# The first load of a log-sum-exp kernel in packets of 4 KB

## The chip, the cores and the metric

The kernel runs on one core of one Trainium2 chip; the other cores are idle. The metric is the device time of one execution in microseconds (us). All views of the profile come from one profiled execution of the kernel.

## What is computed

```python
"x": np.random.randn(32, 512, 1024).astype(np.float32)

def reference(x):
    max_x = np.max(x, axis=-1, keepdims=True)
    return (max_x.squeeze(-1) + np.log(np.sum(np.exp(x - max_x), axis=-1))).astype(np.float32)
```

For each of 16,384 rows of 1024 floats this is the logarithm of the sum of the exponentials. The input is 64 MiB, the output 64 KiB.

## The kernel before

Each of the 128 partitions holds 128 rows. The first 112 rows of a partition are contiguous in HBM (`x_rows`), the last 16 as well (`x_rest`). A ring in SBUF has room for 48 rows for each partition (`RING`), 192 KB.

The list `LOADS` sets the work: 18 loads of 16, 16, 16, 16, 13.5, 12.5, 9 and so on down to 0.46875 rows for each partition, and for each load how its rows are summed. One load is one DMA over all 128 partitions, issued on the queue of SP (SyncE) in `load` (line 139 of the profile). Both sides of it are contiguous within a partition: the first load moves 16 rows, 65,536 bytes, into each partition, and is carried out in one packet for each partition, 128 packets, eight for each of the core's 16 DMA engines. Each DMA engine adds one packet of 4 bytes that counts up the load's semaphore `landed[i]`; 16 such counts make the load landed.

On a landed load ScalarE (ACT) takes the exponential in place (line 228). The maximum isn't subtracted beforehand: the kernel computes the plain sum, checks that every sum and the last row's inputs are in a safe range, and has a slow path for inputs that aren't, which this input doesn't take. The sums go three ways: VectorE (DVE) adds whole rows (`R`, line 239); GpSimd (POOL) first adds the halves of a row (`F`, line 233) and VectorE sums what is left (line 171); or VectorE adds halves and sums in one instruction a row (`T`, line 249). The very last row comes in two pieces (`Y`, `Z`) that ScalarE sums itself (line 202). Logarithms (lines 268, 279, 281), the checks on VectorE and TensorE, and two stores (lines 276, 285) end the kernel.

The order around the change is written out by hand. SP issues the loads in the order of the list, and before an issue `sp.wait` waits for whichever engine last used that part of the ring. Loads 1 to 3 fill the 48 rows and wait for nothing. Load 4 waits until VectorE has summed the first 16 rows. The first load is moved to the front of the program by `start_early`: it stands in SP's first block, ahead of the Drain and the start barrier of the engines, and is the first instruction of the span; loads 2 and 3 are issued behind that barrier.

Of the kernel before, what the change touches and what calls it, by code (L numbers as in the profile page):

```python
# [15 lines left out]
RING = 48  # L16
B = 16
LATE = 119

# [31 lines left out]
def kernel(  # L53
# [30 lines left out]
    def source(e0, size):  # L84
        assert e0 >= W * d or e0 + size <= W * d
        return x_rest[:, e0 - W * d : e0 - W * d + size] if e0 >= W * d else x_rows[:, e0 : e0 + size]
# [8 lines left out]
    def sbuf(name, cols, dtype=fp32, rows=P):  # L95
        return nc.alloc_sbuf_tensor(name, [rows, cols], dtype).ap()

    ring = sbuf("ring", RING * d)
# [35 lines left out]
    def load(i, here, done_before, size):  # L134
        for a, b, who, at in users:
            if a < here + size and b > here:
                sp.wait(who, at)
        users[:] = [u for u in users if not (u[0] < here + size and u[1] > here)]
        return nc.sync.dma_start(
            out=ring[:, here : here + size], in_=source(done_before, size)  # L140
        ).then_inc(landed[i], 16)

    def check_early():
        dve.wait(act, summed_by_act)
        dve.wait(dve, dve.n)
        dve.did(nc.vector.tensor_scalar(  # L146
            out=clamped[:, 0:LATE], in0=sumexp[:, 0:LATE],
            scalar1=LOW, scalar2=HIGH, op0=ALU.max, op1=ALU.min,
        ))
        dve.wait(dve, dve.n)  # L150
        dve.did(nc.vector.scalar_tensor_tensor(  # L151
            out=clamped[:, 0:LATE], in0=clamped[:, 0:LATE], scalar=0.0, in1=sumexp[:, 0:LATE],
            op0=ALU.bypass, op1=ALU.not_equal, accum_out=bad[:, 0:1],
# [4 lines left out]
    def add_up(c, who, **kw):  # L158
        pe.wait(*who)
        return pe.did(nc.tensor.matmul(count, lhsT=ones, rhs=sumexp[:, c : c + 1], **kw))  # L160
# [19 lines left out]
    here = 0  # L180
    early_sum = 0
    done_before = 0
# [3 lines left out]
    for i, (size, ops) in enumerate(loads):  # L186
# [3 lines left out]
        if any(q < here + size and q + t * d > here for _, t, q, _ in folded):  # L190
            reduce_folded()
        dma = load(i, here, done_before, size)
        first_load = first_load or dma.ins
        end = here + size
        done_before += size
        act.wait(landed[i], 16)
        for k, (how, s) in enumerate(ops):
            rows = ring[:, p : p + s * d].rearrange("p (c d) -> p c d", d=d)
            if how in "YZ":
# [3 lines left out]
                    out=last_exp[:, here - p : end - p], in_=ring[:, here:end], func=AF.Exp,  # L203
# [4 lines left out]
                here = end  # L208
# [5 lines left out]
            elif how == "A":  # L214
# [3 lines left out]
                    out=v, in_=v, func=AF.Exp, accum_out=sumexp[:, c : c + 1]  # L218
# [5 lines left out]
            else:  # L224
# [4 lines left out]
                here = upto  # L229
            if how == "F":  # L230
# [3 lines left out]
                    out=rows[:, :, 0:H], in0=rows[:, :, 0:H], in1=rows[:, :, H:d], op=ALU.add  # L234
                ))
                folded.append((c, s, p, at))
            elif how == "R":
                dve.wait(act, at)
                who = (dve, dve.did(nc.vector.reduce_sum(  # L239
                    out=sumexp[:, c : c + s], in_=rows, axis=AX.X  # L240
                )))
                users.append((p, p + s * d, *who))
            elif how == "T":
# [3 lines left out]
                for r in range(s):  # L247
                    lo = rows[:, r, 0:H]
                    who = (dve, dve.did(nc.vector.scalar_tensor_tensor(  # L249
                        out=lo, in0=lo, scalar=1.0, in1=rows[:, r, H:d],  # L250
                        op0=ALU.mult, op1=ALU.add, accum_out=sumexp[:, c + r : c + r + 1],
                    )))
                    users.append((p + r * d, p + (r + 1) * d, *who))
                    if c + r >= LATE:
                        add_up(c + r, who, start=False, stop=False)
            if how == "A" and c >= LATE:
                add_up(c, who, start=False, stop=False)
# [5 lines left out]
            p += s * d  # L263
            if c == LATE:

# [3 lines left out]
                    out=res[:, 0:W], in_=sumexp[:, 0:W], func=AF.Ln  # L269
# [12 lines left out]
        out=res[:, LAST:NC], in_=last_sum, func=AF.Ln, bias=sumexp[:, LAST:NC]  # L282
# [7 lines left out]
    dve.did(nc.vector.scalar_tensor_tensor(  # L290
        out=clamped[:, LATE:NC], in0=sumexp[:, LATE:NC], scalar=LOW,
        in1=sumexp[:, LATE:NC], op0=ALU.max, op1=ALU.not_equal, accum_out=bad[:, 1:2],
# [9 lines left out]
        out=over[:, 0:half], in0=last_piece[:, 0:half], scalar=CEILING,  # L302
# [16 lines left out]
    with nc.If(all_fine < 1):  # L319
# [5 lines left out]
        for c0 in range(0, NC, RING):  # L325
# [6 lines left out]
            for c1, c2 in ((c0, edge), (edge, c0 + s)):  # L332
                if c1 == c2:
                    continue
                nc.scalar.dma_start(
                    out=ring[:, (c1 - c0) * d : (c2 - c0) * d],
                    in_=source(c1 * d, (c2 - c1) * d),
# [4 lines left out]
                out=neg, in_=v, op=ALU.max, axis=AX.X, negate=True  # L342
# [3 lines left out]
                out=v, in0=v, in1=neg[:, :, None].to_broadcast([P, s, d])  # L346
# [5 lines left out]
                out=sumexp[:, c0 : c0 + s], in_=v, axis=AX.X  # L352
# [70 lines left out]
```

## Time and profile before

| | |
|---|---|
| time, median of two runs | 161.68 us (161.67 and 161.69) |
| span of the profiled execution, first to last instruction | 160.39 us |
| its own time | not listed apart from the two runs; median less span 1.29 us |
| busy ACT, DVE, POOL, PE | 114.5, 114.3, 37.3, 2.2 us |
| read from HBM | 67.11 MB, 419 GB/s over the span |
| ScalarE's wait for loads | 43.0 us in 8 waits, the longest 19.3 us |

The span is counted from SP's first instruction, the issue of the first load. Busy time of an engine doesn't count the issuing of DMAs. In a view by stretches the DMA share is the engine time of the packets that start in the stretch, divided by 16 engines times its length; a packet of 64 KB takes longer than a short stretch, so the share can be over 1 there. GB/s is counted in the same way. An entry of the DMA list gives the size of the load and the time from its issue to its landing.

### The profile page before, as it was taken

Reading aid. Unit: us, or ns where it says so; the run is one execution under the profiler, and the core shown is the slowest. Engines: PE = TensorE matmul, PEld = TensorE weight load, DVE = VectorE, ACT = ScalarE, POOL = GpSimd, SP = SyncE. Lnnn points to the kernel's source line nnn. Section 1 sums busy time; section 2 is a strip of 40 time slices with the busy share of each in tenths; the row PEclk is TensorE's granted clock in tenths of the full one; section 3 lists DMA queues with packets and bytes.
Section 4 is the critical chain, followed back from the end, with each engine's and each line's share of the span. In section 5 each row is a group of like instructions: output and inputs, shape, how many; then the busy total and the mean of one; then the engine's idle time right before and its main releaser. Section 6 shows DMA issues by size and latency. Waiting matters only on the chain.

```text
span 160.4 us, 219 instructions
## 1 busy us (share of the span) xinstructions
PE 2.2 (1%) x26; PEld 1.1 (1%) x26; DVE 114.3 (71%) x59; ACT 114.5 (71%) x31; POOL 37.3 (23%) x11
## 2 busy tenths in 40 slices
PE   0000000000000000000000000000000000000022
PEld 0000000000000000000000000000000000000011
DVE  0000000009999499994999859959999999999996
ACT  3000059990699708995099949991999989799996
POOL 0000000000000000000000994690004969891000
DMA  7996996996996996996999999999999999999992
GB/s 262 523 523 262 523 523 262 523 507 278 523 490 294 523 490 294 523 490 294 482 441 441 441 425 409 409 409 480 432 395 417 450 416 398 448 411 424 412 413 95
DMA packets 2881, 67.18 MB, mean 419 GB/s; under 512 B 576, under 2 KB 704, under 8 KB 1344
## 3 DMA queue, kind: packets, MB, share of 16 engines
q1 hardware_dynamic: 2880, 67.18, 97.7%
q14 instruction: 1, 0.01, 0.0%
HBM read 67.11 MB, written 0.07 MB: 419 GB/s over the span
## 4 chain that ended last, share of the span: by engine, by line
DMA 52%; ACT 28%; DVE 19%; issue 1%; PE 0%
DMA ring<-in_x_dram 52%; ACT ring L228 27%; DVE sumexp L239 15%; DVE sumexp L171 2%; DVE ring L249 1%; DVE over L301 0%; PE count L306 0%; ACT res L268 0%; DVE clamped L290 0%; DVE fine L308 0%; DVE sumexp L212 0%
## 5 line engine op out<-in xcount | busy, mean ns | idle before, releaser
L228 ACT ACTIVATE ring<-ring 128x16384 f32<-128x16384 f32 (+16 forms) x23 | 111.7, 4908 | 43.0 <-DMA ring<-in_x_dram 43.0
L239 DVE TENSOR_REDUCE sumexp<-ring 128x16 f32<-128x16384 f32 (+4 forms) x9 | 85.6, 9513 | 42.7 <-ACT ring L228 42.7
L233 POOL TENSOR_TENSOR ring<-ring 128x3072 f32<-128x3072 f32 (+3 forms) x7 | 37.1, 5313 | 107.3 <-ACT ring L228 107.3
L171 DVE TENSOR_REDUCE sumexp<-ring 128x6 f32<-128x3072 f32 (+3 forms) x7 | 18.4, 2656 | 0.0
L249 DVE SCALAR_TENSOR_TENSOR ring<-ring 128x512 f32<-128x512 f32 x15 | 9.6, 687 | 0.4 <-ACT ring L228 0.4
L125 ACT ACT_TABLE_LOAD x1 | 1.3, 1283 | 1.4 <-PEq L62 1.4
L156 PE MATMUL count<-far,bad 128*1 128x1 f32 x2 | 0.2, 164 | 153.2 <-DVE clamped L151 153.2
L160 PE MATMUL count<-sumexp,ones 128*1 128x1 f32 x18 | 1.6, 164 | 3.6 <-DVE ring L249 3.6
L249 DVE DVE_READ_ACCUMULATOR ring<-ring 128x1 f32 x15 | 1.2, 82 | 0.0
L202 ACT ACTIVATE last_exp<-ring 128x544 f32<-128x544 f32 (+1 forms) x2 | 1.2, 584 | 0.0
L126 DVE MEMSET ones<- 128x1 f32 x1 | 0.1, 59 | 1.5 <-PEq L62 1.5
L156 PEld LDWEIGHTS count<-far,bad 128*1 128x1 f32 x2 | 0.1, 80 | 153.2 <-DVE clamped L151 153.2
L160 PEld LDWEIGHTS count<-sumexp,ones 128*1 128x1 f32 x18 | 0.8, 80 | 4.5 <-DVE ring L249 4.5
L301 DVE SCALAR_TENSOR_TENSOR over<-ring 128x240 f32<-128x240 f32 x1 | 0.4, 404 | 0.0
L308 DVE TENSOR_SCALAR fine<-count 1x1 int32<-1x1 f32 x1 | 0.1, 147 | 0.3 <-PE count L306 0.3
L151 DVE SCALAR_TENSOR_TENSOR clamped<-clamped,sumexp 128x119 f32<-128x119 f32 x1 | 0.3, 283 | 0.0
L268 ACT ACTIVATE res<-sumexp 128x112 f32<-128x112 f32 x1 | 0.3, 279 | 0.0
L281 ACT ACTIVATE res<-last_sum,sumexp 128x1 f32<-128x1 f32 x1 | 0.3, 261 | 0.0
L202 ACT ACTIVATION_READ_ACCUMULATOR last_exp<-ring 128x1 f32 x2 | 0.3, 126 | 0.0
L146 DVE TENSOR_SCALAR clamped<-sumexp 128x119 f32<-128x119 f32 x1 | 0.2, 221 | 0.0
L279 ACT ACTIVATE res<-sumexp 128x15 f32<-128x15 f32 x1 | 0.2, 209 | 0.0
L290 DVE SCALAR_TENSOR_TENSOR clamped<-sumexp 128x9 f32<-128x9 f32 x1 | 0.2, 169 | 0.0
(17 smaller groups left out, 1.8 us busy)
## 6 DMA issues: line engine op xcount, KB each, us to landing
ring<-in_x_dram SPq DMA_DIRECT2D x1, 6912.0 KB, 23.9
ring<-in_x_dram SPq DMA_DIRECT2D x1, 6400.0 KB, 19.7
ring<-in_x_dram SPq DMA_DIRECT2D x1, 4608.0 KB, 15.9
ring<-in_x_dram SPq DMA_DIRECT2D x1, 3584.0 KB, 24.0
ring<-in_x_dram SPq DMA_DIRECT2D x1, 3072.0 KB, 19.1
ring<-in_x_dram SPq DMA_DIRECT2D x1, 2288.0 KB, 24.1
ring<-in_x_dram SPq DMA_DIRECT2D x1, 1664.0 KB, 20.9
ring<-in_x_dram SPq DMA_DIRECT2D x1, 1264.0 KB, 23.6
```

The lines of the kernel that those rows point to most:

```text
L125: nc.scalar.preload_act_table_set("natural_log_exp_and_others")
L151: dve.did(nc.vector.scalar_tensor_tensor(out=clamped[:, 0:LATE], in0=clamped[:, 0:LATE], scalar=0.0, in1=sumexp[:, 0:LATE], op0=ALU.bypass ...
L156: pe.did(nc.tensor.matmul(count, lhsT=bad[:, 0:1], rhs=far, start=True, stop=False))
L160: return pe.did(nc.tensor.matmul(count, lhsT=ones, rhs=sumexp[:, c : c + 1], **kw))
L171: at = dve.did(nc.vector.reduce_sum(out=sumexp[:, c0 : c0 + s0], in_=halves, axis=AX.X))
L202: at = act.did(nc.scalar.activation(out=last_exp[:, here - p : end - p], in_=ring[:, here:end], func=AF.Exp, accum_out=first_sum if how == ...
L228: at = act.did(nc.scalar.activation(out=v, in_=v, func=AF.Exp))
L233: at = pool.did(nc.gpsimd.tensor_tensor(out=rows[:, :, 0:H], in0=rows[:, :, 0:H], in1=rows[:, :, H:d], op=ALU.add))
L239: who = (dve, dve.did(nc.vector.reduce_sum(out=sumexp[:, c : c + s], in_=rows, axis=AX.X)))
L249: who = (dve, dve.did(nc.vector.scalar_tensor_tensor(out=lo, in0=lo, scalar=1.0, in1=rows[:, r, H:d], op0=ALU.mult, op1=ALU.add, accum_out ...
L268: ln_early = act.did(nc.scalar.activation(out=res[:, 0:W], in_=sumexp[:, 0:W], func=AF.Ln))
L301: dve.did(nc.vector.scalar_tensor_tensor(out=over[:, 0:half], in0=last_piece[:, 0:half], scalar=CEILING, in1=last_piece[:, half : 2 * half ...
```

## The change

One argument is added to the DMA in `load`: for the first load alone (`i == 0`) the last dimension of the transfer is cut at 4096 bytes, so that each partition's 65,536 bytes are written in 16 packets of 4 KB instead of one of 64 KB. The bytes, their addresses, the queue, the place of the instruction in the program and the semaphore stay as they are. For the other loads `None` leaves the transfer as it was.

```diff
+FIRST_BYTES = 4096
...
         return nc.sync.dma_start(
-            out=ring[:, here : here + size], in_=source(done_before, size)
+            out=ring[:, here : here + size], in_=source(done_before, size),
+            max_dma_last_dim=FIRST_BYTES if i == 0 else None,
         ).then_inc(landed[i], 16)
```

## The prediction

> **What bounds the kernel now.** I read the profile in the order DMA rows, chain of waits, table by stage, waits of the SP queue. The first question is whether the first load lies on the path at all.
>
> ```profile
> span 160.4 us, 219 instructions
> ...
> DMA  7996996996996996996999999999999999999992
> GB/s 262 523 523 262 523 523 262 523 507 278 523 490 294 523 490 294 523 490 294 482 441 441 441 425 409 409 409 480 432 395 417 450 416 398 448 411 424 412 413 95
> DMA packets 2881, 67.18 MB, mean 419 GB/s; under 512 B 576, under 2 KB 704, under 8 KB 1344
> ...
> q1 hardware_dynamic: 2880, 67.18, 97.7%
> ```
>
> The load queue moves 67.18 MB, and its packets fill 97.7% of the time of 16 DMA engines: only 2.3% of 160.4 us, 3.7 us, is without a packet. The swing between 262 and 523 GB/s in the early slices is counting, not idling: a packet is booked whole where it starts. 2880 packets are 20 transfers (18 loads, 2 stores) of 144: eight data packets and one completion packet of 4 bytes for each of 16 engines. Where the 3.7 us lie shows the table by stage (columns: stretch and length, busy time and instructions of PE, PEld, DVE, ACT, POOL, the clock, DMA share, GB/s).
>
> ```profile
> 0.00:1.00 1.00, 0.00 (x0) 0.00 (x0) 0.00 (x0) 0.00 (x0) 0.20 (x4) 1.00 0.00 0
> ...
> 4.00:157.40 153.40, 1.32 (x14) 0.60 (x14) 112.55 (x46) 111.67 (x24) 37.11 (x7) 1.00 1.00 431
> ...
> 158.90:160.39 1.49, 0.19 (x2) 0.09 (x2) 0.15 (x1) 0.03 (x1) 0.00 (x0) 1.00 0.06 6
> ```
>
> The share is 0.00 in the first microsecond, 1.00 from 4.0 to 157.4, and almost nothing at the end. Between first and last load the engines never run dry. The chain and the waits say the same from the other side:
>
> ```profile
> 1.45 39.86 DMA ring<-in_x_dram
> 41.30 0.02 issue
> 41.33 13.87 ACT ring L228
> ...
> 72.46 23.87 DMA ring<-in_x_dram
> ...
> 119.11 19.09 DMA ring<-in_x_dram
> 138.20 0.02 issue
> 138.22 12.34 ACT ring L228 x5
> ```
> ```profile
> 138.22 12.34 ACT L228 ACTIVATE ring<-ring 128x2048 f32<-128x2048 f32 x5 [1.04 <-DMA ring<-in_x_dram]
> ...
> 157.96 0.12 ACT L202 ACTIVATION_READ_ACCUMULATOR last_exp<-ring 128x1 f32 x1
> 158.01 0.56 ACT L202 ACTIVATE last_exp<-ring 128x480 f32<-128x480 f32 x1
> ```
> ```profile
> 0.00 0.39 SPq L139 DMA_DIRECT2D ring<-in_x_dram  x1
> ...
> 1.45 0.84 SPq L139 DMA_DIRECT2D ring<-in_x_dram  x2
> ...
> 53.14 0.33 SPq L139 DMA_DIRECT2D ring<-in_x_dram  x1
> ```
> ```profile
> L139 SPq DMA_DIRECT2D ring<-in_x_dram x18: 327/410/2217, 0.0 to 137.0; - x18
> ...
> DMA to landing us min/median/max: 15.9/22.8/58.8
> ```
> ```profile
> ring<-in_x_dram SPq DMA_DIRECT2D x1, 240.0 KB, 20.9
> ```
>
> The chain goes through ACT and DVE for part of its way, but those pieces set when SP may reuse a part of the ring, not when the engines run out. Load 4, which waits for DVE to free the first 16 rows, is issued at 53.14, while load 3 (one of the two issued between 1.45 and 2.29, with the longest landing, 58.8) arrives after 60.2: its successor is queued 7 us ahead. The last load is issued at 137.0 and lands 20.9 us later, at 157.9; ScalarE takes it at 158.01. Ahead of this, at 138.22, ScalarE had sat 1.04 us waiting for a load. So the end follows the stream of loads in both directions: a stream later by d ends the kernel d later, and one earlier by up to about 1 us still pulls ScalarE with it. What the change does to the first load's time on the engines arrives whole at the end.
>
> **The change part by part.** It removes 128 packets of 65,536 B and adds 2048 of 4096 B: on each engine 8 become 128, the completion packet stays, no byte is added. The price of a packet comes from the tail, where the loads get short. I cut stretches in which the packets that start have one size only; GB/s times length gives bytes and with them the count, and share times 16 times length gives the engine time that they took.
>
> ```profile
> 0.00:4.00 4.00, 0.00 (x0) 0.00 (x0) 0.15 (x4) 1.28 (x1) 0.20 (x4) 1.00 0.76 262
> 4.10:4.75 0.65, 0.00 (x0) 0.00 (x0) 0.00 (x0) 0.00 (x0) 0.00 (x0) 1.00 3.72 1613
> 141.59:141.62 0.03, 0.00 (x0) 0.00 (x0) 0.03 (x1) 0.03 (x1) 0.03 (x1) 1.00 5.69 2441
> 150.78:150.81 0.03, 0.00 (x0) 0.00 (x0) 0.03 (x1) 0.03 (x1) 0.00 (x0) 1.00 2.34 990
> 154.32:154.34 0.02, 0.00 (x0) 0.00 (x0) 0.02 (x2) 0.02 (x1) 0.00 (x0) 1.00 2.91 1190
> ```
>
> Row 4.10: 1613 GB/s x 0.65 us = 1.05 MB, 16 packets of 64 KB; 3.72 x 16 x 0.65 = 38.7 us, 2418 ns each. Row 141.59: 4 packets of 18,304 B (4.46875 rows), 2.73 us, 683 ns each. Row 150.78: 4 of 7424 B, 1.12 us, 281 ns. Row 154.32: 6 of 3968 B, 0.93 us, 155.2 ns. The line through the first and the last is (2418 - 155.2) / (65,536 - 3968) = 0.03675 ns for a byte and 155.2 - 145.8 = 9.4 ns for a packet; the 7424 B row leaves 281 - 272.8 = 8.0 for a packet, the 18,304 B row 10. So a packet costs about 8 to 10 ns whatever its size, and 4096 B are bracketed from both sides by 3968 and 7424 B, hardly an extrapolation.
>
> Sum on one engine: 120 more packets x 8.0 to 9.4 ns = 0.96 to 1.13 us; I take the middle, 1.04. As a check, 128 x (150.5 + 8.7) = 20.4 us against 8 x 2.418 = 19.34 before. All engines pay alike and nothing covers it, since the stream has no gap: **+1.04 us**.
>
> A rule speaks to the same term. The Trainium skill, "DMA: Bandwidth & Descriptors", section on why small descriptors are slow, puts the fixed overhead inside a DMA engine at about 3 cycles for a packet; at the 850 MHz that the page gives, that is an estimated 3.5 ns, and 120 of them 0.42 us, a time of 162.1. This trace shows two to three times as much for a packet, and the sum goes by the trace.
>
> The start of the stream. Row 0.00:4.00 holds the first packet of each engine (262 x 4 = 1.05 MB, 16 packets): 0.76 x 16 x 4 = 48.6 us, 3.04 each against 2.418, so on average 0.62 us goes into getting started. When it goes show these:
>
> ```profile
> 1.00:1.10 0.10, 0.00 (x0) 0.00 (x0) 0.00 (x0) 0.00 (x0) 0.00 (x0) 1.00 8.23 2621
> ...
> 1.70:2.10 0.40, 0.00 (x0) 0.00 (x0) 0.00 (x0) 0.40 (x1) 0.00 (x0) 1.00 0.81 328
> ```
>
> The four that start before 1.10 take 8.23 x 16 x 0.1 / 4 = 3.29 us each, the two that start after 1.70 take 0.81 x 16 x 0.4 / 2 = 2.59. Whoever starts early is held until about the same moment: all second packets begin between 4.10 and 4.75, as if full speed began between 1.7 and 2.3. A loss that ends at a moment, and doesn't come again with packets two to eight, hangs on the beginning and not on the size of a packet; I take it as unchanged, 0. Its bounds: if all engines ran at full speed from 1.02, the slowest would gain 2.33 - 1.02 = 1.3 us; on the other side, 0.6 us more if the loss doubled.
>
> Queueing the packets. The load is still one instruction of SP, but with 128 + 1 entries for each engine instead of 9. What the queue holds shows the end of the loading:
>
> ```profile
> 136.53 2.71 SPq L139 DMA_DIRECT2D ring<-in_x_dram  x2
> ```
>
> The last load's issue took 2.22 us (the maximum of 327/410/2217) while nine loads stood ahead of it: load 9, which the chain shows landing at 138.20, and eight whole ones with 9 entries each, some 73 in all. If that is the room there is, 129 entries leave about 56 to be put in while others drain: 56 x 0.159 = 8.9 us in which SP is held. That costs nothing as long as all engines are fed meanwhile. SP's next issues (loads 2 and 3, from 1.45 on now) must only come before the first load is through at about 22; the start barrier behind it may be late too, since ScalarE idles till then:
>
> ```profile
> 22.00 13.86 ACT L228 ACTIVATE ring<-ring 128x16384 f32<-128x16384 f32 x1 [19.27 <-DMA ring<-in_x_dram]
> ```
>
> The table load (1.3 us) and four memsets have 19 us for themselves. From below the cost is 0; I take 0; the upper end is a rival below. Loads 2 and 3 then follow on each engine without a gap, and the later issues keep their lead of 7 us, since landing, ScalarE and VectorE move together with the stream.
>
> Sum: +1.04 + 0 + 0. The profiled execution spans 160.39 us, 1.29 us less than the median of 161.68, which lies outside the span and which the change doesn't touch; 160.39 + 1.04 = 161.43 of span, and **162.7 us** of time, 0.6% slower.
>
> **The rivals.** First, small packets also mend the start. For: the excess shows in the first packet alone, and a 64 KB piece may have to wait as a whole for something that a 4 KB piece passes. Against: early starters lose most and late ones next to nothing, as with a common gate. At the mean excess, 1.04 - 0.62 = +0.42, 162.1 us; at its extreme 1.04 - 1.3 = -0.26, 161.4 us. Beside it lies that the split isn't carried out (both sides are contiguous, so it could be joined again): 161.7 us.
>
> Second, on the slow side: the entries are handed out engine by engine into the limited room. With 128 entries for the first engines and room for some 73, those that come last get nothing until the first have drained 56: 8.9 us, on which the slowest engine, and with it the landing, is late: 161.7 + 1.0 + 8.9 = 171.6 us, 6% slower. For: the 2.22 us issue shows that room is finite and that the issuer waits for it. Against: the first packets of all 16 engines start within 1.1 us of each other, and the last load was held without any engine falling dry. It decides as slower from the point where the slowest engine gets its first or its next entries more than 2.2 us late (2% is 3.2 us, 1.04 is spent).
>
> Third, a smaller loss of the same place: making 2048 entries instead of 128 delays the first packet, or the start's loss doubles. The first packet starts at 1.02 after an issue of 0.39; 0.6 us more on either ground gives 163.3, and 2 us give 164.7.
>
> **How the numbers follow.** The packet price alone (162.3 to 163.1): 0.53. A mended start or no split (161.4 to 162.3): 0.26. A later start (163.1 to 164.9): 0.12. Handing out in turn (over 164.9): 0.08. Something not seen that gains over 2%: 0.01, since the whole of what the start loses is 1.3 us and 2% is 3.2. The range from 161.5 to 164.0 leaves out the extreme of the mended start, the upper part of the later start, and the handing out in turn, together under 2 in 10. Changes of 2%, about what a measurement of this kernel can tell from none, I count as such: faster 0.01, within 0.91, slower 0.08.
>
> **What would show it.** The profile after should count 2880 - 128 + 2048 = 4800 packets on the queue, the same bytes, and under 8 KB 1344 + 2048 = 3392. A stretch inside the first load should give 158 to 160 ns for a packet (GB/s divided by share 409 to 415, not 433). ScalarE's first exponential should start at 23.0 instead of 22.00, the second at 42.4 instead of 41.33, and each later step about 1.04 us later. The forecast is wrong if ScalarE starts at 22.4 or earlier (the start was mended), if the second load follows the first by more than 19.4 us (queueing reached into it), or if the shift of the first load isn't found at the end.

## The result and the profile after

The changed kernel takes 162.93 us (162.91 and 162.95) against 161.68: +1.25 us, a ratio of 1.0077 with a 95% interval of 1.006 to 1.0093. It is slower by an amount that can be measured, and far within 2%. The forecast was 162.7 with a range of 161.5 to 164.0.

The page of the changed kernel, at the rows that the prediction named:

```profile
span 161.6 us, 219 instructions
...
DMA packets 4801, 67.18 MB, mean 416 GB/s; under 512 B 576, under 2 KB 704, under 8 KB 3392
...
q1 hardware_dynamic: 4800, 67.18, 98.0%
```

4800 packets on the queue instead of 2880, the same bytes, 2048 more packets under 8 KB: the split was carried out as written. ScalarE's rows show where the time went:

```profile
23.17 13.86 ACT L230 ACTIVATE ring<-ring 128x16384 f32<-128x16384 f32 x1 [20.39 <-DMA ring<-in_x_dram]
42.52 13.86 ACT L230 ACTIVATE ring<-ring 128x16384 f32<-128x16384 f32 x1 [5.49 <-DMA ring<-in_x_dram]
61.88 13.86 ACT L230 ACTIVATE ring<-ring 128x16384 f32<-128x16384 f32 x1 [5.50 <-DMA ring<-in_x_dram]
...
159.22 0.56 ACT L204 ACTIVATE last_exp<-ring 128x480 f32<-128x480 f32 x1
```

The first exponential starts at 23.17 instead of 22.00, +1.17. From there on the shift stays: 42.52 against 41.33 (+1.19), and the last piece at 159.22 against 158.01 (+1.21). The chain of waits has the same 33 pieces in the same order, all moved. The loss is made inside the first load and nothing gives it back.

Inside the first load (columns as before: share, then GB/s, at the end of the line):

```profile
0.00:1.10 1.10, 0.00 (x0) 0.00 (x0) 0.00 (x0) 0.00 (x0) 0.20 (x4) 1.00 0.00 0
0.00:2.50 2.50, 0.00 (x0) 0.00 (x0) 0.15 (x4) 1.00 (x1) 0.20 (x4) 1.00 0.54 108
...
4.00:8.00 4.00, 0.00 (x0) 0.00 (x0) 0.00 (x0) 0.00 (x0) 0.00 (x0) 1.00 1.02 420
8.00:21.00 13.00, 0.00 (x0) 0.00 (x0) 0.00 (x0) 0.00 (x0) 0.00 (x0) 1.00 1.03 410
```

From 4 to 8 us 420 x 4 / 0.004096 = 410 packets start, in 1.02 x 64 = 65.3 us of engine time: 159 ns each, the forecast value. From 8 to 21 us it is 410 GB/s and 214 / 1301 = 165 ns. So the price of a packet was met, and then rose once by some 5 ns, which nothing before had shown. A share above 1 means that successive packets of one engine overlap by some nanoseconds; what counts for the stream is GB/s, 16 x 4096 / 420 = 156.0 ns from packet to packet and then 159.8.

SP's queue shows the hold that the prediction had worked out:

```profile
1.50 8.07 SPq L140 DMA_DIRECT2D ring<-in_x_dram  x1
```

The issue of the second load takes 8.07 us instead of 0.33: SP was held while the first load drained. The engines weren't starved: the second exponential follows the first by 19.35 us, as before (19.33).

### The profile page after: what moved, and what is told of

It reads as the page before. It is cut to its first block, busy times and chain, and to the rows that moved or that the text cites. A ratio compares the mean times of both kernels' runs of the same rounds, so it can differ in the third digit from the quotient of the medians.

```text
span 161.6 us, 219 instructions
## 1 busy us (share of the span) xinstructions
PE 2.2 (1%) x26; PEld 1.1 (1%) x26; DVE 114.3 (71%) x59; ACT 114.5 (71%) x31; POOL 37.3 (23%) x11
## 4 chain that ended last, share of the span: by engine, by line
DMA 52%; ACT 27%; DVE 18%; issue 1%; PE 0%
DMA ring<-in_x_dram 52%; ACT ring L230 27%; DVE sumexp L241 15%; DVE sumexp L173 2%; DVE ring L251 1%; DVE over L303 0%; PE count L308 0%; ACT res L270 0%; DVE clamped L292 0%; DVE fine L310 0%; DVE sumexp L214 0%
```

## The experiments

**Theory.** Each added packet costs the engines a fixed time, in whatever load it stands, and the sum arrives at the end because the stream of loads has no gap. **Rivals.** A charge made once at the start, by cutting at all; and a crowded queue, in which the loss comes from the entries that don't fit at once.

The first three experiments change one number of the changed kernel:

```diff
-FIRST_BYTES = 4096
+FIRST_BYTES = 8192      # then 2048, 1024
```

> The first load in packets of 8 KB, 64 for each engine in place of 8. Price by the packet (each added packet costs the same 8.5 to 10 ns): 56 x 8.5 to 10 = 0.48 to 0.56 us, 162.2 us, ScalarE's first exponential at 22.5. Rival, crowded queue (part of the loss comes from the 129 entries not fitting at once, 65 do): no held issue on SP, and only the early pace of the changed kernel's load, about 5.4 ns for a packet: 0.3 us, 162.0 us. Rival, start (the loss is made once, in the first two microseconds, by cutting at all): 162.9 us again.

> The first load in packets of 2 KB, 256 for each engine. Price by the packet: 248 x 8.5 to 10 = 2.1 to 2.5 us, 163.8 to 164.2 us. SP's issue of the second load is held about twice as long as the 8.1 us with 4 KB, since twice the entries at half the time each exceed the room: (257 - 80) x 0.084 = 15 us, at no cost of its own. The change of pace that the changed kernel's load shows at 8 us (159 to 164 ns for a packet) comes at 8 us if it hangs on the clock, at some 5 us if it hangs on the number of entries used, at some 15 us if it comes when the last entry has been put in. Start: 162.9 us.

> The first load in packets of 1 KB, 512 for each engine. Price by the packet: 504 x 8.5 to 10 = 4.3 to 5.0 us, 166.0 to 166.7 us, and SP's issue of the second load held about 18 us, still before the first load is through. If putting in the entries is slower than using them (one for 16 engines every 2.9 ns would be needed), the loss is out of proportion, over 167 us, and the engines show gaps. Start: 162.9 us.

| first load's packets | added for each engine | time | more than before | for each added packet |
|---|---|---|---|---|
| 8 KB | 56 | 162.17 us | 0.60 us (1.0035, 1.0021 to 1.0049) | 10.7 ns |
| 4 KB (the change) | 120 | 162.93 | 1.25 | 10.4 |
| 2 KB | 248 | 163.98 | 2.41 (1.0145, 1.0128 to 1.0162) | 9.7 |
| 1 KB | 504 | 166.43 | 4.86 (1.0300, 1.0282 to 1.0317) | 9.6 |

The kernel before took 161.57 us on the chip of these three, and 161.68 on that of the change. The loss is very nearly proportional to the packets. Between 8 KB and 1 KB it is (166.43 - 162.17) / 448 = 9.5 ns for a packet, and 0.05 to 0.1 us remain that don't depend on their number. The traces say the same: ScalarE's first exponential starts at 22.41, 24.32 and 26.60, a slope of (26.60 - 22.41) / 448 = 9.4 ns. The start as the cause would have given the same time for all four and is refuted. SP's issue of the second load was held 13.92 us with 2 KB and 19.25 with 1 KB and not at all with 8 KB (0.84 us for loads 2 and 3 together, as before); the rows for 2 KB and 1 KB, one kernel each:

```profile
1.50 13.92 SPq L140 DMA_DIRECT2D ring<-in_x_dram  x1
```
```profile
1.50 19.25 SPq L140 DMA_DIRECT2D ring<-in_x_dram  x1
```

Holding SP longer didn't raise the price of a packet (9.7 and 9.6 ns), so the held queue costs nothing by itself. The rival of the crowded queue expected 162.0 with 8 KB, which wasn't met, but the 0.2 us between it and 162.2 is near what such runs scatter; the pace decides it. With 8 KB, where everything fits and nothing is held:

```profile
4.00:12.00 8.00, 0.00 (x0) 0.00 (x0) 0.00 (x0) 0.00 (x0) 0.00 (x0) 1.00 1.01 428
13.00:21.00 8.00, 0.00 (x0) 0.00 (x0) 0.00 (x0) 0.00 (x0) 0.00 (x0) 1.00 1.01 422
```

The pace drops here too, from 16 x 8192 / 428 = 306.2 to 310.6 ns for a packet. Crowding isn't what makes the later packets slower.

**Another load.** The second load is cut and the first is left whole.

```diff
-            max_dma_last_dim=FIRST_BYTES if i == 0 else None,
+            max_dma_last_dim=FIRST_BYTES if i == 1 else None,
```

> The second load in packets of 4 KB, the first as before in 64 KB: the queue is already running and the start untouched. Price by the packet: the same +1.0 to 1.2 us, 162.7 to 162.9 us, ScalarE's first exponential at 22.0 as before, the second late by the whole amount (42.4). Start: no loss, 161.7 us.

162.81 us, ratio 1.0074 (1.0057 to 1.0091): +1.24, what the change itself costs.

```profile
22.07 13.86 ACT L230 ACTIVATE ring<-ring 128x16384 f32<-128x16384 f32 x1 [19.33 <-DMA ring<-in_x_dram]
42.53 13.86 ACT L230 ACTIVATE ring<-ring 128x16384 f32<-128x16384 f32 x1 [6.61 <-DMA ring<-in_x_dram]
61.90 13.86 ACT L230 ACTIVATE ring<-ring 128x16384 f32<-128x16384 f32 x1 [5.50 <-DMA ring<-in_x_dram]
```
```profile
1.45 27.28 SPq L140 DMA_DIRECT2D ring<-in_x_dram  x2
```

The first exponential is where it was; the second load takes 42.53 - 22.07 = 20.46 us instead of 19.33, +1.13; the third follows at the old distance. The start has no part in it. SP was held for most of 27 us with loads 2 and 3, again at no cost.

**A charge for cutting at all, and several cut loads.** Packets of 32 KB add only eight to each engine; in the other kernel loads 1 to 3 are all cut to 4 KB (`if i <= 2`).

> The first load in packets of 32 KB, 16 for each engine in place of 8. Price by the packet: 8 x 9.6 to 10.7 = 0.08 us, hardly more than the runs scatter. A charge for cutting at all, which the runs with 1 to 8 KB leave room for at 0.05 to 0.1 us, would bring it to 0.13 to 0.18 us. Start mended by smaller pieces: faster than before by up to 0.5 us.

> Loads 1, 2 and 3 all in packets of 4 KB, three times 120 more packets for each engine. Price by the packet: three times the 1.2 us of one load, +3.6 us, and each of ScalarE's first three exponentials another 1.13 to 1.17 us later: 23.2, 43.6, 64.1. If part of the 1.2 us were a charge made once, the sum would be less, some 3 us. SP is held for most of the time until the third load is put in, some 28 us, still ahead of its next issue at about 53.

32 KB: 161.86 us against 161.66, +0.20, ratio 1.0018 (1.0009 to 1.0027). Eight packets pay 0.08 of it; some 0.1 us remains, a small charge made once, in line with the 0.05 to 0.1 left above. Part of it may lie at the very start: SP's issue of a cut first load takes longer.

```profile
0.00 0.44 SPq L140 DMA_DIRECT2D ring<-in_x_dram  x1
```

It was 0.39 before, and in the changed kernel no packet starts before 1.10 (its first row above), against 1.02. But the kernel with the second load cut keeps as much (1.24 - 120 x 0.0095 = 0.10), with its first load issued as before, so where the charge is made isn't shown. A mended start is refuted: this kernel would have been the one to gain. Three cut loads: 165.22, +3.56 us for 360 packets, 9.9 ns each (1.0222, 1.0206 to 1.0237), and the exponentials at 23.26, 43.73 and 64.20, at distances of 20.47 each. The prices add up.

**Does the end follow the first load?** The kernel before, with the one line left out that moves the first load ahead of the barrier:

```diff
-    nc.at_finalize(start_early)
```

> The kernel before, with the first load issued behind the start barrier, as loads 2 and 3 are, instead of ahead of it. No change of packets. If whatever delays the first load arrives whole at the end, ScalarE's first exponential and the end are late by the same amount, about 1.1 to 1.45 us (the issue moves from 0 to where load 2 stood). If the kernel has slack behind the first load, the end moves less than the first exponential.

163.03 us against 161.65, +1.38 (1.0083, 1.0068 to 1.0098). The issue is at 1.39 instead of 0, the rest follows:

```profile
23.22 13.86 ACT L228 ACTIVATE ring<-ring 128x16384 f32<-128x16384 f32 x1 [20.54 <-DMA ring<-in_x_dram]
42.55 13.86 ACT L228 ACTIVATE ring<-ring 128x16384 f32<-128x16384 f32 x1 [5.48 <-DMA ring<-in_x_dram]
...
159.24 0.56 ACT L202 ACTIVATE last_exp<-ring 128x480 f32<-128x480 f32 x1
```

First exponential +1.22, last +1.23: what reaches the first exponential of a delay that has nothing to do with packets arrives whole at the end too.

**A stream with gaps.** With `RING = 40` only two loads of 16 rows fit, and the engines wait for VectorE between the pairs of loads. Three kernels in five runs: this alone, twice; with the second load cut, twice; with the first load cut, once.

> The kernel before with a ring of 40 rows in place of 48, so that only two loads of 16 rows fit and load 3 must wait until VectorE has summed the first at 53.1. No change of packets. It is slow by design: the stream stands still from about 41 to 54 and again later. It serves as the base for the next run.

> The same ring of 40 rows, with the second load in packets of 4 KB. If the price is paid at the end only where the stream of loads has no gap behind the cut load: the second load lands 1.1 us later and ScalarE's second exponential starts 1.1 us later, but load 3 waits for the sum of the first load in any case, and the end moves by under 0.3 us against the ring of 40 alone. If the cut costs its 1.2 us wherever it stands, the end is 1.2 us later.

> The ring of 40 rows without cut packets once more, as the base of the two next on the same chip: 190.8 us.

> The ring of 40 rows, the first load in packets of 4 KB. The first load stands at the head of the chain (its sum frees the ring for load 3), so its 1.2 us should arrive at load 3 and at the end whole: 192.0 us, ScalarE's third exponential 1.2 us later than in the base.

> The ring of 40 rows, the second load in packets of 4 KB, again, because the first look found +0.67 us at the end with runs 0.8 us apart, while its trace had the whole price gone at load 3. Cover by the gap: the end clearly less late than with the first load cut, by some 0.7 us or more; ScalarE's third exponential where the base has it, apart from a shift that the first exponential has too.

The times are 190.84 alone and 191.51 with the second load cut in the first set; 190.97 (190.08 to 192.07) alone, 191.94 (191.83 to 192.69) with the first cut and 191.53 (191.24 to 192.11) with the second cut in the other. The runs of one kernel lie up to 2 us apart here, so that the time doesn't separate 0.3 from 1.2 us: by the times the question stays open, and the expectation of under 0.3 was missed at +0.67 and +0.56. With the first load cut the end is +0.97 late, as expected, but that is only 0.41 more than with the second cut, where 0.7 or more was expected. The traces are clearer up to the fifth exponential. First the base, then the second load cut:

```profile
21.96 13.86 ACT L228 ACTIVATE ring<-ring 128x16384 f32<-128x16384 f32 x1 [19.23 <-DMA ring<-in_x_dram]
41.30 13.86 ACT L228 ACTIVATE ring<-ring 128x16384 f32<-128x16384 f32 x1 [5.48 <-DMA ring<-in_x_dram]
74.89 13.86 ACT L228 ACTIVATE ring<-ring 128x16384 f32<-128x16384 f32 x1 [19.74 <-DMA ring<-in_x_dram]
94.24 13.95 ACT L228 ACTIVATE ring<-ring 128x9216 f32<-128x9216 f32 x2 [5.49 <-DMA ring<-in_x_dram]
124.99 11.82 ACT L228 ACTIVATE ring<-ring 128x6144 f32<-128x6144 f32 x2 [16.80 <-DMA ring<-in_x_dram]
```
```profile
22.13 13.86 ACT L230 ACTIVATE ring<-ring 128x16384 f32<-128x16384 f32 x1 [19.39 <-DMA ring<-in_x_dram]
42.53 13.86 ACT L230 ACTIVATE ring<-ring 128x16384 f32<-128x16384 f32 x1 [6.55 <-DMA ring<-in_x_dram]
75.28 13.86 ACT L230 ACTIVATE ring<-ring 128x16384 f32<-128x16384 f32 x1 [18.89 <-DMA ring<-in_x_dram]
95.81 13.95 ACT L230 ACTIVATE ring<-ring 128x9216 f32<-128x9216 f32 x2 [6.67 <-DMA ring<-in_x_dram]
125.11 11.82 ACT L230 ACTIVATE ring<-ring 128x6144 f32<-128x6144 f32 x2 [15.35 <-DMA ring<-in_x_dram]
```

Counted from the first exponential, the second is at 19.34 and with the cut at 20.40 (+1.06); the third at 52.93 and 53.15 (+0.22); the fourth at 72.28 and 73.68 (+1.40); the fifth at 103.03 and 102.98 (-0.05). The two traces of the first set give +1.13, -0.02, +1.26 and +0.13. Load 3 waits for the sum of the first load, and the price of the second is nearly covered there; load 4 waits for the sum of the second, and the price is back; load 5 waits for the third, and it is gone. With the first load cut the shift of the first exponential, +1.35, is carried on whole to the third, at nearly the same distance (52.86 against 52.93):

```profile
23.31 13.86 ACT L230 ACTIVATE ring<-ring 128x16384 f32<-128x16384 f32 x1 [20.53 <-DMA ring<-in_x_dram]
...
76.17 13.86 ACT L230 ACTIVATE ring<-ring 128x16384 f32<-128x16384 f32 x1 [19.65 <-DMA ring<-in_x_dram]
```

So a price in a load is covered where the next transfer waits for something else, and not where it heads the chain. From the sixth exponential on, the two traces of the uncut kernel themselves differ by some 0.5 us, and how much of the price reaches the end of this kernel isn't shown.

## Why the prediction was right, point by point

**What bounds the kernel** held. The end follows the first load: +1.17 at the first exponential became +1.21 at the last piece, and the late first load showed the same without any packets (+1.22 and +1.23).

**The price of a packet** was right in kind and somewhat small in size: 8.0 to 9.4 ns forecast, 9.5 measured over 448 packets. The term of +1.04 should have been 120 x 9.5 = 1.14. That it came so near is in part luck. The rows of the tail gave the duration of a packet, 159 ns with 4 KB, and the first ones took just that long; but they overlap, and at their pace of 156.0 ns from packet to packet the load would have cost only 128 x 0.156 - 19.33 = 0.64 us. What brings it back is the drop of the pace after some 40 packets of an engine, which the prediction didn't have. From packet to packet, 39 up to 8.0 us ((222 x 4 + 420 x 4) GB/s us / 4096 B / 16, with 222 GB/s from 0 to 4 us) at 156.0 and 89 at 159.8 ns make 20.31 us, 0.98 more than the 19.33 of a whole load.

```profile
0.00:4.00 4.00, 0.00 (x0) 0.00 (x0) 0.15 (x4) 1.28 (x1) 0.20 (x4) 1.00 0.72 222
```

**The start** was taken as unchanged, and no change is shown. The 66 packets that start before 2.50 in the changed kernel take 0.54 x 40 = 21.6 us, 11.1 more than 66 x 0.159, or 0.69 us for each engine against 0.62. But with the second load cut, where the first is whole, the share from 0 to 4 us is 0.81, which by the sum of the prediction is 0.81 x 4 - 2.42 = 0.82: traces differ by more than these 0.07. With the first packet 0.08 later, 0.98 + 0.08 = 1.06 of the 1.17 us at the first exponential have a place. The other 0.11 I can't place; in six traces with a whole first load issued at 0 that exponential starts anywhere from 21.71 to 22.13. The loss isn't tied to a moment of the execution, 1.7 to 2.3 us, as the prediction could be read: in the kernel with the late first load, the five packets that start before 2.50 still take 5.00 x 16 x 0.20 / 5 = 3.2 us each. It comes with the beginning of the stream.

```profile
2.30:2.50 0.20, 0.00 (x0) 0.00 (x0) 0.00 (x0) 0.20 (x1) 0.00 (x0) 1.00 5.00 1638
```

**The queue** held: a hold of 8.9 us was forecast and 8.07 came, at no cost. It fell on the issue of the second load and not on that of the first, which took 0.44 us. When it ended, at 9.57, each engine had used some 49 packets ((222 x 4 + 420 x 4 + 410 x 1.57) / 65.5) and not 56, so by the same reckoning the room would be about 80 entries instead of 73.

**The rivals.** The mended start (0.26) is refuted by the four sizes and by 32 KB, none of which gains. Handing out in turn (0.08) is refuted by 1 KB: 513 entries for each engine, and still all engines fed, at 9.6 ns for a packet. That the split isn't carried out, counted with the first, is refuted by the 4800 packets. Of the later start (0.12) the first packet's 0.08 us is true.

**The rule on small packets.** The Trainium skill, "DMA: Bandwidth & Descriptors", section on why small descriptors are slow, gives about 3 cycles for a packet, an estimated 3.5 ns at its 850 MHz. The runs show 9.5 ns, so this overhead alone would have put the loss at a third of what it is. Only before the drop is the trace near it: 156.0 - 19,330 / 128 = 5.0 ns for a packet, and 8.8 after it.

## What to carry to other kernels

Where the profile shows the DMA engines full from first load to last, every packet costs its time (here 9.5 ns on each engine, the same in loads 1 to 3), and cutting a load into more packets is paid in full. The price of a packet can be read beforehand from loads of different lengths in the same trace: cut stretches with one size, divide share by GB/s, and draw the line. That is an estimate: here it gave 8.0 to 9.4 ns, and couldn't show that the first few dozen packets of a cut load are cheaper. Before counting on a cover, ask whether the next transfer waits for the dearer one or for something else.

## What the runs showed of the hardware that was not expected

The pace of cut loads drops once, after a few dozen packets of each engine: a packet then takes 4 to 5 ns more, whatever its size, from 156.0 to 159.8 ns with 4 KB and from 306.2 to 310.6 with 8 KB (rows above), and from 16 x 2048 / 410 = 79.9 to 84.7 with 2 KB (first two rows) and from 42.9 to 47.1 with 1 KB (last two):

```profile
2.50:5.00 2.50, 0.00 (x0) 0.00 (x0) 0.00 (x0) 0.28 (x1) 0.00 (x0) 1.00 1.05 410
6.00:23.00 17.00, 0.00 (x0) 0.00 (x0) 0.00 (x0) 0.00 (x0) 0.00 (x0) 1.00 1.05 387
```
```profile
2.50:4.00 1.50, 0.00 (x0) 0.00 (x0) 0.00 (x0) 0.28 (x1) 0.00 (x0) 1.00 1.07 382
6.00:24.00 18.00, 0.00 (x0) 0.00 (x0) 0.00 (x0) 0.00 (x0) 0.00 (x0) 1.00 1.10 348
```

It comes between 5 and 6 us with 2 KB, at 8 us with 4 KB and between 12 and 13 us with 8 KB, so it hangs on the packets used and not on the clock, though not on one fixed count; and it comes without a held issue as well (8 KB). With the second load cut, it comes inside the second load:

```profile
22.50:26.00 3.50, 0.00 (x0) 0.00 (x0) 0.00 (x0) 3.50 (x1) 0.00 (x0) 1.00 1.02 420
28.00:41.00 13.00, 0.00 (x0) 0.00 (x0) 5.05 (x1) 7.92 (x1) 0.00 (x0) 1.00 1.03 410
```

With three loads cut it doesn't come a second time: loads 2 and 3 run at the lower pace (409 GB/s from 24 to 62 us). Its cause is open, and so is what in an engine takes the time of a packet.

The issue behind a load with many entries holds SP, for 8.07 us with 4 KB, 13.92 with 2 KB and 19.25 with 1 KB, and it is the next load's issue that is held and not that of the load with the many entries. That the room in the queue is limited is the likely reason; no run varies it.
